# Delta rule: inverses and output weights pass through DRAM rings, decays are made by ScalarE

## The chip, the cores and the metric

The program runs on one core of one Trainium2 chip. The metric is device time in microseconds (us), from the first to the last instruction of the core and the little that lies around it. The engines are TensorE (PE in the profile; PEld are its weight loads), VectorE (DVE), ScalarE (ACT), GpSimd (POOL) and SyncE (SP). SP does no arithmetic: it issues transfers (DMAs), in order, and waits before one whose data or place is not ready. ACT issues some DMAs too.

## The reference, cut to what matters

One layer of a hybrid backbone: 1024 latent tokens and 256 context tokens, width 1024. One projection feeds two branches. Branch B is a differential softmax attention of 8 heads; branch A, where the change lies, is a gated delta rule of 8 heads with keys and values of 128, run over the tokens in both directions. For each head and direction it goes chunk by chunk:

```python
gc = jnp.cumsum(chunks(g), axis=-1)
decay = jnp.where(incl, jnp.exp(jnp.where(incl, gc[..., :, None] - gc[..., None, :], 0.0)), 0.0)
a_mat = jnp.where(strict, jnp.einsum('nbhid,nbhjd->nbhij', kc * bc[..., None], kc) * decay, 0.0)
t_mat = lax.linalg.triangular_solve(eye + a_mat, jnp.broadcast_to(eye, a_mat.shape), left_side=True, lower=True)
...
qk = jnp.where(incl, jnp.einsum('nbhid,nbhjd->nbhij', qc, kc) * decay, 0.0)
...
def step(s, xs_i):
    v_new = u_i - jnp.einsum('bhck,bhkv->bhcv', w_i, s)
    s_next = s * jnp.exp(gl_i)[..., None, None] + jnp.einsum('bhck,bhcv->bhkv', kd_i, v_new)
    o = jnp.einsum('bhck,bhkv->bhcv', qd_i, s) + jnp.einsum('bhij,bhjv->bhiv', qk_i, v_new)
```

The inverse of each chunk (`t_mat`) and the output weights (`qk`) don't depend on the state and can be made ahead of the scan over the chunks. Afterwards both branches are normed, gated, projected, merged and projected again.

## The kernel before

The kernel takes chunks of 128 tokens: 10 of them (`NT`), of which 8 are latent (`NL`). It runs in this order: norm and modulation, the projections of attention, of keys and of values (to about 660 us), then the delta rule together with the rest of the projections, then attention, and at the end the output projections.

In the delta-rule part (`run`, lines 721 to 741) several streams (Python generators) each yield one instruction at a time with its engine, an assumed duration and what it depends on. `flow` (line 86) takes the stream whose next instruction could start first, by assumed clocks of the engines, and so writes out a fixed order for PE, DVE, ACT, POOL and SP. On the chip each engine then works through its list in order and waits where a value is late. A DMA is assumed to take its own duration after the one before it and 2.0 us more. The streams:

- `scan(0)` and `scan(1)` (line 1180): the two directions, one head after the other, ten chunks each. A chunk is a chain of PE (`kT`, state S), DVE (`r`), PE (the inverse, `X[:, d, c]`), ACT (`vd`), PE (`kk`), DVE (new S). `out_chunk` (line 1227) makes the chunk's output from `qT`, `qk` and S in a queue of its own.
- `preps(0)` and `preps(1)` (line 1006): preparation of the even and of the odd heads, `gdn_prep` (line 1011). Steps: loads of a row of `gc`, spread over the partitions, into X (L1022), of kT and qT (L1024, L1025); decays in X: direction 0 by ten DVE steps (L1033), direction 1 by two POOL operations (L1028, L1030), then Exp of each; Gram products on PE, and their products with the decays on DVE, into `qk` and X (L1052, L1056); the diagonal blocks of 32 x 32 through DRAM (`da`, L1066 to L1079) to a layout with one block per partition, 31 steps of substitution on DVE (L1084, L1086), and back through DRAM (`db`, L1088, L1094); the merge of the block inverses to 64 and 128 by small matmuls (`pz`, `p2`, `p3`, `pz6`, `pu6`) with copies and memsets into X (L1104 to L1164); the scaling by beta (L1167); loads of kk and vv (L1174, L1175).
- `tails` (line 1248): norm and gate of a head's output; it ends with two stores.
- The filler: the projections of 6 query columns and of 32 gate columns, 48 matmuls each (`fill_flow`, tile `mm`), whose weights ACT loads and ACT and POOL split into two parts (`wh`, `wl`, L827 to L833). The filler has the lowest priority, and what is left of it when the last tail is done runs while attention begins (`rest`, line 155).

Each of the two pools `gh[0]` and `gh[1]` holds X, qk, kT and qT of one head, from the loads to the end of its scan. So `preps` waits for `min(self.scanned) > h - 2`: both directions of head h - 2 must be scanned. Two flags (`busy`, `merging`) let only one head at a time be in the substitution and one in the merge.

```python
yield lambda: self.gh[s] and C_Q + h * P in self.filled and min(self.scanned) > h - 2
```

Of the kernel before, what the change touches and what calls it, by code (L numbers as in the profile page):

```python
# [8 lines left out]
F32 = mybir.dt.float32  # L9
# [16 lines left out]
H = 8  # L26
# [33 lines left out]
class Block:  # L60
# [136 lines left out]
    def setup(self):  # L197
# [31 lines left out]
        self.ma = self.dp.tile([KT, P, L], F32, name="ma")  # L229
        self.gcd = self.dp.tile([2 * H, LT], F32, name="gcd")  # L230
# [437 lines left out]
    def run(self):  # L668
# [4 lines left out]
        with ExitStack() as left:  # L673
            self.hp, self.hs = self.spool(left, "hp"), {}
            self.hgroup(0)
            with ExitStack() as lw, ExitStack() as cx:
# [13 lines left out]
                with ExitStack() as sv:  # L690
# [30 lines left out]
                    with tc.manual_schedule(engines={E.PE, E.DVE, E.Activation, E.Pool, E.SP}):  # L721
# [243 lines left out]
    def gdn_first(self, st, keep):  # L965
# [3 lines left out]
        self.banks, self.busy, self.merging = [], False, False  # L969
        self.gs = None  # L970
        self.over, self.kvover, self.zring = {}, [[], []], [[], []]
        self.aT, self.ready, self.scanned, self.read, self.tailed = {}, {}, [0, 0], [0, 0], 0
        self.outq = [[], []]
# [32 lines left out]
    def preps(self, s):  # L1006
        for h in range(s, H, 2):
            yield lambda: self.gh[s] and C_Q + h * P in self.filled and min(self.scanned) > h - 2
            yield from self.gdn_prep(h)

    def gdn_prep(self, h):
# [3 lines left out]
        kT, qT = G("kT", [P, LT]), G("qT", [P, L])  # L1015
        X = G("X", [P, 2, NT, P])
        qk = G("qk", [P, 2, NL, P])
        ld = [None] * 2
        old = self.over.get(h - 2, [])
        for d in range(2):  # L1020
# [3 lines left out]
        tk = yield DMA, 1.82, old, lambda: nc.sync.dma_start(kT, self.gk[h])  # L1024
        tq = yield DMA, 1.46, old, lambda: nc.sync.dma_start(qT, self.gq[h])  # L1025
        te = [None] * 2
        g = H + h
        t = yield POOL, 2.28, [ld[1]], lambda: nc.gpsimd.tensor_tensor(  # L1028
            X[:, 1], self.gcc[:, :, g].unsqueeze(2).to_broadcast([P, NT, P]), X[:, 1], ALU.subtract)
        t = yield POOL, 2.84, [t], lambda: nc.gpsimd.tensor_tensor(X[:, 1], X[:, 1], self.sg.unsqueeze(1).to_broadcast(  # L1030
            [P, NT, P]), ALU.mult)
        for c in range(NT):
            t0 = yield DVE, 0.33, [ld[0]], lambda: V.scalar_tensor_tensor(X[:, 0, c], X[:, 0, c], self.gcc[:, c, h:h + 1],  # L1033
                                                                         self.sg, ALU.subtract, ALU.mult)
        te[0] = yield ACT, 1.16, [t0], lambda: nc.scalar.activation(X[:, 0], X[:, 0], AF.Exp), AF.Exp
        te[1] = yield ACT, 1.16, [t], lambda: nc.scalar.activation(X[:, 1], X[:, 1], AF.Exp), AF.Exp

        tX, tQ = [[], []], [[], []]
        for c0 in range(0, NT, 2):
# [10 lines left out]
            for d in range(2):  # L1050
                if c0 < NL:
                    t1 = yield DVE, 0.42, [t, te[d]], lambda: V.tensor_tensor(qk[:, d, c0:c0 + 2], pv[:, :, 1],  # L1052
# [17 lines left out]
        for d in range(2):  # L1070
            t = yield POOL, 2.303, tQ[d], lambda: nc.gpsimd.tensor_tensor(
                qk[:, d], qk[:, d], (self.up, self.lo)[d].unsqueeze(1).to_broadcast([P, NL, P]), ALU.mult)
            tQ[d] = t
        yield lambda: not self.busy
        self.busy = True
# [13 lines left out]
        self.busy = False  # L1089
        yield lambda: not self.merging  # L1090
        self.merging = True
# [4 lines left out]
        t64 = self.t64  # L1096
# [11 lines left out]
        self.banks.append(tz)  # L1108
        yield self.psum(2)
# [8 lines left out]
        tx = []  # L1118
        for m in range(4):
            tx += [(yield DVE, 0.48, [tt], lambda: V.tensor_copy(X[B(m), 0, :, B(m)], Rt[B(m), 0:NT]))]  # L1120
            tx += [(yield ACT, 0.46, [tt], lambda: nc.scalar.copy(X[B(m), 1, :, B(m)], R[B(m), NT:]))]
        for (b1, b2) in ((0, 1), (2, 3)):
            tx += [(yield POOL, 0.41, [tz], lambda: nc.gpsimd.memset(X[B(b2), 0, :, B(b1)], 0.0))]
            tx += [(yield POOL, 0.41, [tz], lambda: nc.gpsimd.memset(X[B(b1), 1, :, B(b2)], 0.0))]
# [6 lines left out]
        tx.append(t)  # L1131
        self.banks.append(t)
# [3 lines left out]
        for (m, q, f) in ((0, slice(0, 32), R[B(0), 0:NT]), (1, slice(32, 64), R[B(1), 0:NT]), (2, slice(0, 32), Rt[B(2), NT:]),  # L1136
                          (3, slice(32, 64), Rt[B(3), NT:])):
            t6 += [(yield DVE, 0.36, [tt], lambda: V.tensor_copy(t64[B(m), :, q], f))]
# [31 lines left out]
        self.merging = False  # L1170
        yield lambda: self.gs and (h == 0 or min(self.read) >= h - 1)
        kk, vv = (self.gs.tile([P, NT, P], F32, tag=n, name=n) for n in ("kk", "vv"))
        yield lambda: h == 0 or min(self.read) >= h
# [692 lines left out]
```

## Time and profile before

| | us |
|---|---|
| three runs | 2163.01, 2168.39, 2171.24; median 2168.39 |
| the profiled execution, its own time | 2171.22 |
| its span, first to last instruction | 2169.4 |
| PE busy | 2031.0 (94%) |
| DVE, ACT, POOL busy | 1494.5 (69%), 965.1 (44%), 988.0 (46%) |
| moved by DMA | 300.77 MB, mean 139 GB/s |

The profile times every instruction of one execution. "Busy" is time in which an engine executes; waiting, branching and issuing a DMA do not count. PEclk is the share of full clock that TensorE was granted. In a row of the time line stand start, duration, engine, line, operation, what it writes `<-` what it reads, and in brackets how long the engine was idle before and what released it. A row of the waits gives the waiting and the releasing instruction, total us, times, and the longest. Most matmuls are issued by one helper, so their line is L71, and the name of the tile tells them apart. Matmuls overlap each other: their rate is read from their starts.

### The profile page before, as it was taken

Reading aid. Unit: us, or ns where it says so; the run is one execution under the profiler, and the core shown is the slowest. Engines: PE = TensorE matmul, PEld = TensorE weight load, DVE = VectorE, ACT = ScalarE, POOL = GpSimd, SP = SyncE. Lnnn points to the kernel's source line nnn. Section 1 sums busy time; section 2 is a strip of 40 time slices with the busy share of each in tenths; the row PEclk is TensorE's granted clock in tenths of the full one; section 3 lists DMA queues with packets and bytes.
Section 4 is the critical chain, followed back from the end, with each engine's and each line's share of the span. In section 5 each row is a group of like instructions: output and inputs, shape, how many; then the busy total and the mean of one; then the engine's idle time right before and its main releaser. Section 6 shows DMA issues by size and latency. Waiting matters only on the chain. (4 is left out here: it accounts for less than half of the span.)

```text
span 2169.4 us, 37611 instructions
## 1 busy us (share of the span) xinstructions
PE 2031.0 (94%) x14207; PEld 1704.1 (79%) x14207; DVE 1494.5 (69%) x3492; ACT 965.1 (44%) x1979; POOL 988.0 (46%) x685
## 2 busy tenths in 40 slices
PE   8999999998899688888999899899999999999999
PEld 4999998887798577767787678686777777777899
DVE  4867776876777787885868767335788888873532
ACT  4322222434432344544355345246777777773210
POOL 2265663132335425443453433434776676775122
PEclk9999999999999799989999999999999999999999
DMA  9323335666665324334344432627455466217443
GB/s 318 97 80 127 108 107 176 169 167 173 189 173 156 98 79 124 109 113 126 98 144 128 131 118 86 189 88 226 105 143 139 129 165 176 93 55 255 145 143 97
DMA packets 351304, 300.77 MB, mean 139 GB/s; under 512 B 140063, under 2 KB 299393, under 8 KB 351123
## 3 DMA queue, kind: packets, MB, share of 16 engines
q1 hardware_dynamic: 304867, 254.85, 40.1%
q10 hardware_dynamic: 46256, 43.52, 6.4%
q8 instruction: 112, 1.84, 0.4%
q14 instruction: 69, 0.57, 0.1%
HBM read 200.64 MB, written 97.68 MB: 138 GB/s over the span
## 5 line engine op out<-in xcount | busy, mean ns | idle before, releaser
L71 PE MATMUL mm<-hs,wh 128*128 128x512 f32 x1216 | 435.9, 423 | 0.8 <-ACT zo L907 0.8
L454 PE MATMUL mm<-wh,hs 128*128 128x256 f32 (+1 forms) x1632 | 305.5, 287 | 0.4 <-DVE abt L656 0.3
L1384 DVE TENSOR_SCALAR_CACHE_REDUCE S<-s 128x512 f32<-128x512 f32 (+1 forms) x384 | 223.2, 597 | 108.7 <-PE s L71 107.9
L71 PEld LDWEIGHTS mm<-hs,wh 128*128 128x128 f32 x1216 | 235.7, 198 | 43.3 <-issue 1.4
L71 PE MATMUL mm<-hs,wl 128*128 128x512 f32 x608 | 256.6, 422 | 8.8 <-POOL wl L833 8.8
L454 PEld LDWEIGHTS mm<-wh,hs 128*128 128x128 f32 x1632 | 258.3, 193 | 1.1 <-DVE abt L656 0.6
L431 PE MATMUL mm<-hs,wh 128*128 128x512 f32 (+1 forms) x832 | 227.8, 361 | 14.2 <-ACT xc L471 14.2
L1414 POOL TENSOR_TENSOR S<-S 128x1280 f32<-128x1280 f32 x64 | 188.6, 2947 | 111.6 <-ACT S L1409 109.1
L454 PE MATMUL mm<-wl,hs 128*128 128x256 f32 (+1 forms) x816 | 232.9, 286 | 0.0
L833 POOL TENSOR_TENSOR wl<-wr,wh 128x512 fp32r<-128x512 f32 x74 | 107.7, 1476 | 175.4 <-ACT wh L832 147.6
L431 PEld LDWEIGHTS mm<-hs,wh 128*128 128x128 f32 x832 | 149.4, 192 | 40.2 <-ACT xc L471 17.0
L1395 ACT ACTIVATE S<-S,mn 128x1280 f32<-128x1280 f32 x128 | 175.0, 1367 | 12.4 <-DVE mn L1388 11.6
L454 PEld LDWEIGHTS mm<-wl,hs 128*128 128x128 f32 x816 | 157.3, 193 | 0.0
L431 PE MATMUL mm<-hs,wl 128*128 128x512 f32 (+1 forms) x416 | 149.7, 360 | 0.0
L71 PEld LDWEIGHTS mm<-hs,wl 128*128 128x128 f32 x608 | 119.9, 197 | 29.5 <-POOL wl L833 9.3
L1430 ACT CAST ah<-t 128x512 fp32r<-128x512 f32 (+1 forms) x192 | 98.3, 513 | 98.8 <-PE t L74 96.2
L71 PE MATMUL s<-kh,qs 128*128 128x512 f32 (+1 forms) x384 | 133.2, 386 | 1.0 <-DVE S L1384 0.8
L476 DVE SCALAR_TENSOR_TENSOR ac<-xc,smallT,ac 128x1284 f32<-128x1284 f32 (+1 forms) x72 | 122.0, 1695 | 12.8 <-ACT ac L472 10.8
L1084 DVE TENSOR_TENSOR tmp<-ab,ts 80x31 f32<-80x31 f32 (+15 forms) x248 | 107.9, 435 | 16.6 <-DMA ab<-da 11.6
L1437 DVE TENSOR_TENSOR al<-t,ah 128x512 fp32r<-128x512 f32 (+1 forms) x192 | 113.6, 592 | 7.8 <-ACT ah L1430 7.3
L74 PE MATMUL t<-ct,S 128*128 128x128 f32 x640 | 101.9, 273 | 8.1 <-DVE al L1437 7.2
L1086 DVE TENSOR_TENSOR ts<-ts,tmp 80x31 f32<-80x31 f32 (+15 forms) x248 | 103.7, 418 | 4.8
(317 smaller groups left out, 5070.6 us busy)
## 6 DMA issues: line engine op xcount, KB each, us to landing
wr<-in_w_in_dram SPq DMA_DIRECT2D x21, 1024.0 KB
wr<-in_w_in_dram ACTq DMA_DIRECT2D x37, 512.0 KB
X<-gcd SPq DMA_DIRECT2D x16, 640.0 KB
kh<-kd SPq DMA_DIRECT2D x32, 320.0 KB
wa<-in_w_ada_dram SPq DMA_DIRECT2D x8, 1024.0 KB
qd<-col SPq DMA_DIRECT2D x16, 512.0 KB
kd<-col SPq DMA_DIRECT2D x16, 512.0 KB
gt<-zo ACTq DMA_DIRECT2D x16, 512.0 KB
```

The source lines that it names most:

```text
L71: self.nc.tensor.matmul(out, lhsT, rhs, start=start, stop=stop)
L74: self.nc.tensor.transpose(out, src, self.ident[:src.shape[0], :src.shape[0]])
L431: nc.tensor.matmul(pt[:, :n], wt[:, k, cs], ht[:, k, o:o + n], start=i == 0, stop=i == 3 * KT - 1)
L454: nc.tensor.matmul(pt[:, j * W:j * W + n], ht[:, k, ts], wt[:, k, :n], start=i == 0, stop=i == 3 * KT - 1)
L476: nc.vector.scalar_tensor_tensor(ac[:, w], xc[:, o + j:o + j + wd // parts], self.convw(j, ct), ac[:, w], ALU.mult, ALU.add)
L833: t2 = yield POOL, 1.36, [t1], lambda: nc.gpsimd.tensor_tensor(lo[:, k], raw[:, k], hi[:, k].bitcast(F32), ALU.subtract)
L1084: t = yield DVE, n * w / 960.0 + 0.11, [t, t1], lambda: V.tensor_tensor(tv, ab[:, j + 1:, j:j + 1].to_broadcast([80, n, w]), ts[:, j, :w]. ...
L1086: t = yield DVE, n * w / 960.0 + 0.11, [t, t1], lambda: V.tensor_tensor(ts[:, j + 1:, :w], ts[:, j + 1:, :w], tv, ALU.subtract)
L1384: self.nc.vector.tensor_scalar(x[c][:, o:o + m], x["s", j, c][:, :m], 1.0, None, ALU.mult, ALU.min, accum_out=x["m3"][:, c, j:j + 1])
L1395: self.nc.scalar.activation(S, S, AF.Exp, bias=x["mn"][:, c:c + 1], scale=-1.0, accum_out=w["l0"][:, c, t:t + 1])
L1414: self.nc.gpsimd.tensor_tensor(x[0], x[0], x[1], ALU.add)
L1437: self.nc.vector.tensor_tensor(y["al", k][:, :, q], x["t", k][:, :nb * P].rearrange("p (j f) -> p j f", f=P), y["ah", k][:, :, q].bitcast( ...
```

## The change

- The decays: for each head and direction ten ScalarE `Abs` (of the loaded row less `gc` of the partition) and one `Exp` with scale -1, in place of the subtraction and the sign on DVE and POOL.
- After the merge each half of X (five chunks, both directions) is stored to `xd` in DRAM, and `qk`, once masked, to `qkd`. The new streams `loads(0)` and `loads(1)` bring them back for the scans in units of two chunks, in rings of two units for each direction; `used_` tells when a unit has been read.
- The new stream `sets` loads the scan's own keys and queries (`sk`, `sq`) with kk and vv, once the head before has been scanned. The kT, qT and qk of preparation lie in `gh[0]` only, one head at a time (`gram`, `kT_t`, `qk_t`); `gh[1]` holds X and the output.
- Preparation of head h waits for `stored > h - 2`. Counters (`subst`, `merge`, `gram`) replace the flags and put the heads in order.
- The masking of qk on POOL (`masked`) and the copies of block inverses into X and t64 (`placed`) run as streams of their own (`asides`), and the four copies out of `p2` depend on its matmuls only.

```diff
@@ run
-    (self.preps(1), 3), (self.tails(), 3), (self.forever(self.convs), 4)):
+    (self.preps(1), 3), (self.tails(), 3), (self.sets(), 3), (self.loads(0), 3), (self.loads(1), 3), (self.forever(self.convs), 4), (self.forever(self.asides[0]), 3),
+    (self.forever(self.asides[1]), 3)):
@@ preps
-            yield lambda: self.gh[s] and C_Q + h * P in self.filled and min(self.scanned) > h - 2
+            yield lambda: self.gh[s] and C_Q + h * P in self.filled and self.stored > h - 2
@@ gdn_prep
-        t = yield POOL, 2.28, [ld[1]], lambda: nc.gpsimd.tensor_tensor(
-            X[:, 1], self.gcc[:, :, g].unsqueeze(2).to_broadcast([P, NT, P]), X[:, 1], ALU.subtract)
-        t = yield POOL, 2.84, [t], lambda: nc.gpsimd.tensor_tensor(X[:, 1], X[:, 1], self.sg.unsqueeze(1).to_broadcast(
-            [P, NT, P]), ALU.mult)
-        for c in range(NT):
-            t0 = yield DVE, 0.33, [ld[0]], lambda: V.scalar_tensor_tensor(X[:, 0, c], X[:, 0, c], self.gcc[:, c, h:h + 1],
-                                                                         self.sg, ALU.subtract, ALU.mult)
-        te[0] = yield ACT, 1.16, [t0], lambda: nc.scalar.activation(X[:, 0], X[:, 0], AF.Exp), AF.Exp
-        te[1] = yield ACT, 1.16, [t], lambda: nc.scalar.activation(X[:, 1], X[:, 1], AF.Exp), AF.Exp
+        for d in range(2):
+            for c in range(NT):
+                t = yield ACT, 0.265, [ld[d]], lambda: nc.scalar.activation(
+                    X[:, d, c], X[:, d, c], AF.Abs, bias=self.gcc[:, c, d * H + h:d * H + h + 1], scale=-1.0)
+            te[d] = yield ACT, 1.18, [t], lambda: nc.scalar.activation(X[:, d], X[:, d], AF.Exp, scale=-1.0), AF.Exp
+        yield lambda: self.gram == h
...
-        yield lambda: not self.busy
-        self.busy = True
+        self.kT_t = [tX[1][-1], list(tQ)]
+        self.asides[0].append(self.masked(h, qk, tQ))
+        yield lambda: self.subst == h
...
-                    t = yield DVE, 0.5, [t], lambda: V.tensor_copy(X[B(r), d, :, B(q)], p2[B(r)])
+                    tx += [(yield DVE, 0.5, [e], lambda: V.tensor_copy(X[B(r), d, :, B(q)], p2[B(r)]))]
                 else:
-                    t = yield ACT, 0.43, [t], lambda: nc.scalar.copy(X[B(r), d, :, B(q)], p2[B(r)])
+                    tx += [(yield ACT, 0.43, [e], lambda: nc.scalar.copy(X[B(r), d, :, B(q)], p2[B(r)]))]
...
+            self.store_t.setdefault(h, []).append((yield DMA, 2.2, ends, lambda: nc.sync.dma_start(
+                self.xd[h][:, :, cs], X[:, :, cs])))
+        self.merge = self.stored = h + 1
+
+    def masked(self, h, qk, tQ):
+        nc, t = self.nc, [None] * 2
+        for d in range(2):
+            t[d] = yield POOL, 2.303, tQ[d], lambda: nc.gpsimd.tensor_tensor(
+                qk[:, d], qk[:, d], (self.up, self.lo)[d].unsqueeze(1).to_broadcast([P, NL, P]), ALU.mult)
+        t = yield DMA, 3.1, t, lambda: nc.sync.dma_start(self.qkd[h].rearrange("p d c f -> p (d c f)"),
+                                                       qk.rearrange("p d c f -> p (d c f)"))
+        self.store_t.setdefault(h, []).append(t)
+        self.qk_t, self.gram = [t], h + 1
...
+    def sets(self):
+        for h in range(H):
+            yield lambda: self.gs and min(self.scanned) >= h and self.tailed >= h - 1 and C_Q + h * P in self.filled
...
+            for n, src in (("sk", self.gk[h]), ("kk", self.gkk[h]), ("vv", self.gv[h]), ("sq", self.gq[h])):
...
+                w["t" + n] = yield DMA, 1.82, free, lambda: nc.sync.dma_start(
+                    o, src.rearrange("(c p) f -> p c f", p=P) if n == "vv" else src)
+
+    def loads(self, d):
+        nc, i = self.nc, 0
+        order = ((8, 0, 2, 4, 6), (8, 6, 4, 2, 0))[d]
+        for h in range(H):
+            for c in order:
+                yield lambda: self.gs and self.stored > h and len(self.used_[d]) > i - 2
+                u = {}
+                for n, src in (("x", self.xd), ("qk", self.qkd))[:2 if c < NL else 1]:
+                    u[n] = x = self.gs.tile([P, 2, P], F32, tag=f"{n}{d}", name=n, bufs=2)
+                    u["t" + n] = yield DMA, 0.45, [self.store_t[h], self.used_[d][i - 2] if i > 1 else None], \
+                        lambda: nc.sync.dma_start(x, src[h][:, d, c:c + 2])
+                self.units_[d, h, c] = u
+                i += 1
@@ scan
-                t = yield PE, 0.2235, [tr, w["tX"]], lambda: self.mm(pc[:, 1], X[:, d, c], r)
+                t = yield PE, 0.2235, [tr, u["tx"]], lambda: self.mm(pc[:, 1], u["x"][:, c % 2], r)
@@ out_chunk
-        t2 = yield PE, 0.2235, [tn, w["tqk"], b], lambda: self.mm(po[:, 1], w["qk"][:, d, c], vn)
+        t2 = yield PE, 0.2235, [tn, u["tqk"], b], lambda: self.mm(po[:, 1], u["qk"][:, c % 2], vn)
@@ tails
             if end:
+                yield lambda: self.stored == H
                 yield from self.att_load_ops(0)
```

More of the change, by code (lines that the diff above doesn't have):

```diff
@@ L1108, in gdn_prep @@
         self.banks.append(tz)
+        tZ.append(tz)
         yield self.psum(2)
@@ L1117, in gdn_prep @@
             t3 = yield PE, 0.02, [tz, b], lambda: self.mm(p3[B(2), c], Z[B(3), c], Rt[B(3), NT + c]), 0.25
[L1118 to L1124, printed above, removed]
+        tx, e = [], t
         for i, (b1, b2) in enumerate(((2, 3), (0, 1))):
@@ L1169, in gdn_prep @@
                 ends.append(t)
[L1170 to L1173, printed above, removed]
-        tkk = yield DMA, 1.82, self.kvover, lambda: nc.sync.dma_start(kk.rearrange("p c f -> p (c f)"), self.gkk[h])
-        tvv = yield DMA, 1.82, self.kvover, lambda: nc.sync.dma_start(vv, self.gv[h].rearrange("(c p) f -> p c f", p=P))
@@ new lines, in placed @@
+    def placed(self, X, R, Rt, tt, tz, out):
+        nc, V, t64 = self.nc, self.nc.vector, self.t64
+        B = lambda b: slice(32 * b, 32 * b + 32)
+        tx, t6 = [], []
+        for m in range(4):
+            tx += [(yield DVE, 0.48, [tt], lambda: V.tensor_copy(X[B(m), 0, :, B(m)], Rt[B(m), 0:NT]))]
+            tx += [(yield ACT, 0.46, [tt], lambda: nc.scalar.copy(X[B(m), 1, :, B(m)], R[B(m), NT:]))]
+        for (m, q, f) in ((0, slice(0, 32), R[B(0), 0:NT]), (1, slice(32, 64), R[B(1), 0:NT]), (2, slice(0, 32), Rt[B(2), NT:]),
+                          (3, slice(32, 64), Rt[B(3), NT:])):
+            t6 += [(yield DVE, 0.36, [tt], lambda: V.tensor_copy(t64[B(m), :, q], f))]
+        yield lambda: tz
+        for (b1, b2) in ((0, 1), (2, 3)):
+            tx += [(yield POOL, 0.41, tz, lambda: nc.gpsimd.memset(X[B(b2), 0, :, B(b1)], 0.0))]
+            tx += [(yield POOL, 0.41, tz, lambda: nc.gpsimd.memset(X[B(b1), 1, :, B(b2)], 0.0))]
+        out += [tx, t6]
```

84 lines of the change are left out of this document (48 added, 36 removed).

## The prediction

> **What bounds the kernel now.** I read four views: the stages, the reasons for which TensorE (PE) sat idle, the waits of SP's queue, and the time line around the largest stall. First the stages: the delta rule with its filler, its last part, and the attention.
>
> ```profile
> span 2169.4 us, 37611 instructions
> PEclk9999999999999799989999999999999999999999
> ...
> core 0: us, PE busy (x) PEld busy (x) DVE busy (x) ACT busy (x) POOL busy (x), PEclk, DMA share, GB/s
> 680.00:760.00 80.00, 59.11 (x499) 47.91 (x498) 65.66 (x151) 29.43 (x43) 39.60 (x29) 0.81 0.40 117
> 760.00:1440.00 680.00, 617.56 (x5087) 513.47 (x5085) 482.58 (x1279) 299.59 (x777) 286.14 (x280) 0.95 0.39 117
> 1440.00:1500.00 60.00, 59.22 (x266) 45.13 (x265) 14.78 (x52) 26.93 (x50) 22.80 (x15) 1.00 0.60 169
> 1500.00:1952.00 452.00, 441.12 (x2683) 329.07 (x2682) 365.44 (x1187) 331.87 (x549) 315.48 (x153) 1.00 0.47 133
> ...
> 1440.00:1500.00 60.00, 51.39 (x208) 1.00 0.60 169
> ```
>
> The last row is the third stretch for the filler's matmuls (`mm`) alone. The scans end near 1440 us, and the filler still has 51.39 us of PE work left; it then runs with PE full (59.22 of 60) at clock 1.00. So the delta-rule part does not end when its scans end: it ends when PE has done its work. The change adds and removes no matmul, so only PE's losses can move: idle time, 80 - 59.11 = 20.9 us and 680 - 617.56 = 62.4 us, and slow clock, 0.19 x 80 = 15 us and 0.05 x 680 = 34 us. Together 132 us at most (the two overlap a little). That is the ceiling of any gain here.
>
> Where does PE sit idle, and what holds preparation?
>
> ```profile
> PE pu L71 <- DVE Z L1152: 13.6, 6, 5.3
> PE oT L74 <- POOL oa L1273: 10.6, 2, 5.9
> PE p L71 <- issue: 9.0, 3, 4.2
> PE mm L71 <- POOL wl L833: 8.8, 1, 8.8
> PE pz L71 <- DVE RR L1095: 7.4, 2, 5.2
> PE chain L71 <- DVE S L1221: 6.5, 7, 2.6
> PE pz L71 <- issue: 5.5, 1, 5.5
> ...
> SPq L1088 <- DVE ts L1086: 190.7, 8, 51.4
> ...
> SPq L1022 <- PE chain L71: 78.9, 4, 39.9
> ...
> SPq L1022 <- PE out L71: 51.1, 2, 27.7
> ...
> L1219 DVE COPY S<-chain x16: 279/282/293, 768.2 to 1410.9; 128x128 f32<-128x128 f32 x16
> ```
>
> Columns of a wait: total us, times, longest. The long idle times belong to the merges (pz, p, pu: 13.6 + 9.0 + 7.4 + 5.5 = 35.5 us), one tail (oT) and one weight split (wl); the scans' own waits are short. SP waits 78.9 + 51.1 = 130 us for scans before it may issue the load of a decay buffer (L1022): preparation of head h+2 starts only after the scan of head h. The first state copies of the heads (L1219) run from 768.2 to 1410.9 us: 642.7 / 7 = 92 us a head. The last head shows the loop:
>
> ```profile
> 1277.18 0.81 SPq L1022 DMA_DIRECT2D X<-gcd  x2
> ...
> 1328.06 4.65 DMA da<-cb
> 1332.78 3.16 DMA ab<-da
> ...
> 1399.20 10.20 PE mm L71 x44
> 1409.40 0.45 PE chain L71 x4
> ...
> 1441.14 13.40 PE mm L71 x59
> ```
>
> Its preparation takes 1409.4 - 1277.2 = 132 us and its scan 32 us. Two buffers take turns, so a mean cycle of 92 us means 184 us for preparation and scan of one buffer.
>
> **The change part by part.** (a) *Decays.* Per head it removes ten DVE steps (L1033) and two POOL operations (L1028, L1030) and adds twenty ScalarE Abs of 128x128; the two Exp stay.
>
> ```profile
> 692.42 2.49 POOL L1028 TENSOR_TENSOR X<-gcc,X 128x1280 f32<-128x1280 f32 x1 [2.71 <-DVE ts L1086]
> 694.99 3.01 POOL L1030 TENSOR_TENSOR X<-X,sg 128x1280 f32<-128x1280 f32 x1
> 698.85 13.59 POOL L833 TENSOR_TENSOR wl<-wr,wh 128x512 fp32r<-128x512 f32 x2 [0.86 <-ACT wh L832]
> ...
> 692.28 0.42 DVE L1084 TENSOR_TENSOR tmp<-ab,ts 80x256 f32<-80x256 f32 x1
> 692.73 2.46 DVE L1086 TENSOR_TENSOR ts<-ts,tmp 80x256 f32<-80x256 f32 x1
> 695.22 3.05 DVE L1084 TENSOR_TENSOR tmp<-ab,ts 80x255 f32<-80x255 f32 x1
> ...
> 711.27 0.80 PE L71 MATMUL mm<-hs,wl 128*128 128x512 f32 x1 [8.83 <-POOL wl L833]
> 711.86 1.05 PE L71 MATMUL mm<-hs,wh 128*128 128x512 f32 x2
> ...
> 714.42 1.05 PE L71 MATMUL mm<-hs,wh 128*128 128x512 f32 x2
> ...
> 1292.22 2.47 POOL L833 TENSOR_TENSOR wl<-wr,wh 128x512 fp32r<-128x512 f32 x2
> ...
> 1009.64 2.71 DVE L1033 SCALAR_TENSOR_TENSOR X<-X,gcc,sg 128x128 f32<-128x128 f32 x10
> ...
> L1208 ACT ACTIVATE vd<-chain,edk 128x128 f32<-128x128 f32 x144 | 51.7, 368 | 78.8 <-PE chain L71 78.2 <-ACT vn L1212 0.2 <-ACT oa L1238 0.2
> ```
>
> Two substitution steps of DVE that take 0.42 us apart took 2.46 and 3.05 us beside these two POOL operations: 4.7 us lost a head, and 2.7 us for L1033 itself (ten in 2.71). The other way round, while L1033 and the query convolution kept DVE full, two weight splits on POOL took 13.59 us, where a pair takes 2.47 at another place; PE waited 8.83 us, and its next matmuls came 0.43 us apart (six from 711.86 to 714.42) instead of 0.23 (59 in 13.40 us, above). The slow stretch adds an estimated 2 us: ten to twelve matmuls at 0.2 us more. ScalarE pays at most 20 x 0.368 = 7.4 us a head (from L1208, the same shape with an operand per partition), 59 us for eight: hidden, since ScalarE is busy 299.6 of 680 us. Uncovered, it would lengthen a preparation by that less the 5.5 us that the two POOL operations took.
>
> The Trainium skill, SBUF — State Buffer (Who interferes with whom), says that DVE and GpSimd share one pair of ports as an exclusive lock, and that a DVE instruction with two SBUF inputs is shut out by a GpSimd instruction that reads SBUF, but not one with a single SBUF input. The 2.46 us above agrees; by the rule nothing of the scans' DVE steps, which read PSUM and one SBUF tile, is relieved, and the term (a2) below would be nearer its small end, at -8, for a sum of 2151 us instead of 2143.
>
> The start (a1), 680 to 760 us: with two POOL operations fewer before the split, I take 8 of the 11 us (8.8 + 2) back; bounds 0 and -11. The heads (a2): 7.4 us less DVE for each of seven heads is 52 us; DVE is the longest of the side engines there (482.6 of 680), yet PE is kept going by filler, so I take less than a third, -16; bounds 0 and -52.
>
> (b) *Buffers.* X goes to DRAM after the merge and comes back in rings of two chunks; so preparation h+2 waits for the store of X by h, no longer for the scan of h. The loop of one buffer loses a scan of 32 us and gains a store, taken as the 4.65 us of `da<-cb`: (184 - 32 + 5) / 2 = 78.5 us a head. DVE needs 482.6 / 680 x 92 = 65 us a head, 7.4 less after (a), 58: under 78, but near enough that I take 80. The scan stage becomes 7 x 12 = 84 us shorter, and the filler that it no longer covers runs after it with PE full, as 1440:1500 shows. The loss rate was (62.4 + 34) / 680 = 14%, so 84 us fewer of such a stage save 12 us; bounds -40 (the loss halves, as merges find scan work beside them) and +30 (the same stalls packed closer, and 5% more).
>
> (c) *Traffic.* Per head X (1.31 MB) and qk (1.05 MB) are written and read back, and kT and qT are loaded twice: 5.9 MB, 47 MB in all, with 18 loads, 3 stores and 2 reloads: 23 issues on SP, 184 in all. SP's issues take 0.3 to 0.45 us, so 55 to 83 us of a queue that waits most of the time. The engines moved 362 GB/s where they were full:
>
> ```profile
> 1284.00:1288.00 4.00, 4.00 (x35) 3.11 (x34) 0.91 (x2) 2.23 (x10) 3.95 (x4) 1.00 1.05 362
> ...
> DMA packets 111185, 96.74 MB, mean 121 GB/s; under 512 B 42339, under 2 KB 93539, under 8 KB 111113
> ```
>
> so 47 MB cost 130 us of transfer beside the 0.39 share now: room enough. A ring load has the time of one unit, 6.4 us (two of ten chunks in 32 us), and lands like `ab<-da` in 3.2 us. It is on the path only at a head's first unit or where SP holds it. I take 1 us of PE a head, +8; bounds 0 and +88 (below).
>
> (d) *Merge order.* The copies into X and t64 move to a stream of their own and the four copies out of p2 no longer wait for each other: no instruction more. Part of (b)'s low bound; 0.
>
> Sum against the profiled execution (2171.2 us for a span of 2169.4; the runs' median is 2168.4, 3 lower): -8 - 16 - 12 + 8 = -28, that is 2143, and 2140 beside the median. I say 2142.
>
> **The rivals.** *Long stalls go (2107).* The merges now have another head's scan beside them, so that PE's long waits become short. The five long kinds above (pu, oT, p, wl, pz twice) are 54.9 us and the slow clock 49; half of both is 52, with 12 of (b): 2171 - 64 = 2107. For it: the scans' own waits are at most 2.6 us each. Against it: a merge's chain from DVE to PE and back is as long as before.
> The Trainium skill, TensorE: Matmul & The Clock Gate (Part 1), puts the slow clock down to idle windows of about 3.4 us; by that rule stalls of 2 us cost their own time only, and all 49 us of clock could go, for about 2110 us. The trace fits it at 711 us, after the 8.83 us stall.
>
> *Nothing is gained (2165).* The order of PE is written out beforehand and its losses come from steps that run later than ordered; with scan, two preparations and merge closer together, DVE (58 of 80 us) is as late as before and the 132 us only move. Only (a1) stays: 2171 - 8 + 2. The same comes out if the new counters (one Gram part, one substitution, one merge at a time) hold preparation where the scan held it.
>
> *Ring loads behind SP (slower, 2209).* SP issues in order. Its store after the substitution (L1088) holds it 190.7 us in 8 waits, up to 51.4 us. Today nothing inside a scan hangs on SP; afterwards nine loads of each direction and head do, and one ordered behind a late L1088 stops the scan's matmul on PE and the filler behind it. Such a stop costs what the 8.83 us one did, 11 us with its clock. In six of eight heads: 66 - 28 = +38, 2209; in all eight 88 - 28 = +60, 2231. It decides from the third stop on (28 / 11).
> The Trainium skill, DMA: Bandwidth & Descriptors (Anatomy of one DMA), gives a DMA about 2 us of fixed cost, most of it the receipt of the write, longest towards HBM; a way through DRAM pays it twice, an estimate of 4 us a head by the page. The rows have 4.65 + 3.16 us for such a pair.
>
> **How the numbers follow.** Chances: forecast 0.40, long stalls go 0.15, nothing gained 0.15, SP 0.30. A measurement here tells 0.5% (11 us) from no change. Faster: 0.37 of the forecast's 0.40, the 0.15, and 0.01: 0.53. Same: 0.03 + 0.13 = 0.16. Slower: 0.30 + 0.01 = 0.31. The forecast's own range is 2120 to 2163. For 8 in 10 I reach down to 2095 (most of the 2107 case) and up to 2200 (half of the slower case).
>
> **What would show it.** Right: no L1028, L1030, L1033; substitution steps near 0.42 us; the first state copies under 85 us apart; SP no longer waiting for the chain at the decay load; after the last scan more than 51 us of filler with PE full; PE's idle time in the stage under 83 us. Wrong: new rows of PE waiting for x or qk from DRAM with several us each (SP), a clock under 0.9 over the stage, or heads 90 us apart (counters). If DVE is over 85% busy and PE waits for it, (b) was too hopeful; if the long merge waits are gone, (b) was too careful.

## The result, and the profile after

The changed kernel takes 2167.3 us (median of 20 runs, 2156.7 to 2174.7) against 2166.6 us before (20 runs): ratio 1.0001, 95% interval 0.9988 to 1.0014. The forecast was 2142; its rival "nothing is gained" had 2165. The profiled execution is the slowest of the 20 (2174.7 us). One execution of a kernel further down (keys buffered once) took 3173 us at a granted clock of 0.556; the medians are without it.

The windows of the changed kernel, columns as before (stretch; busy us of PE, its weight loads, DVE, ACT, POOL; granted clock; DMA share; GB/s):

```profile
680.00:760.00 80.00, 72.78 (x551) 58.16 (x549) 69.17 (x167) 33.46 (x61) 22.19 (x26) 0.91 0.58 179
760.00:1440.00 680.00, 624.23 (x5111) 521.28 (x5107) 459.57 (x1181) 333.06 (x888) 260.62 (x266) 0.95 0.58 183
1440.00:1500.00 60.00, 58.15 (x253) 41.38 (x251) 23.58 (x83) 27.20 (x62) 21.84 (x18) 0.84 0.63 187
1480.00:1500.00 20.00, 19.09 (x50) 9.63 (x49) 12.69 (x50) 12.21 (x17) 9.58 (x4) 0.52 1.07 321
```

PE's idle time in the stage fell from 83.3 to 7.2 + 55.8 = 63.0 us, and DVE has 23 us less. But 1480 to 1500 is new: PE counts as busy, at clock 0.52. The time line of PE shows why:

```profile
1474.74 0.39 PE L71 MATMUL mm<-hs,wl 128*128 128x512 f32 x1
1474.97 0.62 PE L71 MATMUL s<-kh,qs 128*128 128x512 f32 x2
...
1493.69 1.06 PE L74 MATMUL t<-ct,S 128*128 128x128 f32 x4
```

The last filler matmul (`mm`) starts at 1474.7, 24 us earlier than before (1498.5). Attention's first scores (`s`) then run alone for 18.7 us, until the first transposes (`t`) follow; before, filler covered this. So of 24 us only 6 arrive at the first `t` (1499.7 before). No long stall precedes the slow clock: the longest idle gap of PE between 1474.7 and 1493.7 us is 0.48 us.

The rest of the difference lies at the end. Most of the lead is kept until the last scores of attention (4.7 us earlier than before), and the rest, mostly the output projections, which the change does not touch, takes 234.6 us instead of 226.5. Over all profiled executions of this document it takes 225.5 to 234.6 us, so these 8 us are not read as an effect of the change.

The waits of the changed kernel, 680 to 1500 us (total, times, longest), PE's and then SP's:

```profile
PE pu L71 <- DVE Z L1151: 12.2, 5, 4.4
PE pq L71 <- DVE qss L954: 10.2, 3, 4.3
PE chain L71 <- DMA x<-xd: 9.2, 4, 4.2
PE chain L71 <- ACT vd L1262: 6.2, 4, 4.5
...
SPq L1227 <- PE chain L71: 112.2, 41, 10.6
SPq L1348 <- POOL oa L1346: 100.8, 12, 27.8
SPq L1169 <- POOL X L1166: 81.8, 11, 16.6
SPq L1093 <- DVE ts L1091: 29.0, 5, 18.9
```

The stall at the weight split is gone, the merge waits (`pu`) are not. Scans now wait for X from DRAM. SP no longer sits before the store of the substitution (29.0 instead of 190.7 us) but before ring loads whose place is not free (L1227) and stores of X (L1169); it waits for the tails' stores (L1348) as it did before (173.3 us at L1291).

From the same traces, head by head: the preparation (first load of X to last beta; mean of heads 2 to 7), the gap from the last beta to the scan's first matmul (all heads), the gap from the last beta to the next load of X into that buffer, the scan's length, the distance of the scans' starts, and the end of the last scan:

```
                    prep   beta>scan  beta>next X  scan   apart  last scan ends
before             145.1      2.1        39.2      36.3    91.8      1440
after              167.4     19.9         6.8      42.4    88.9      1449
```

### The profile page after: what moved, and what is told of

It reads as the page before. It is cut to its first block, busy times and chain, and to the rows that moved or that the text cites. A ratio compares the mean times of both kernels' runs of the same rounds, so it can differ in the third digit from the quotient of the medians.

```text
span 2172.9 us, 37989 instructions
## 1 busy us (share of the span) xinstructions
PE 2051.0 (94%) x14207; PEld 1719.1 (79%) x14207; DVE 1480.2 (68%) x3412; ACT 1003.2 (46%) x2133; POOL 938.1 (43%) x669
## 5 line engine op out<-in xcount | busy, mean ns | idle before, releaser
L71 PE MATMUL mm<-hs,wh 128*128 128x512 f32 x1216 | 421.5, 418 | 2.0 <-ACT zo L910 1.8
L71 PEld LDWEIGHTS mm<-hs,wh 128*128 128x128 f32 x1216 | 234.6, 196 | 44.7 <-ACT zo L910 2.4
L433 PE MATMUL mm<-hs,wh 128*128 128x512 f32 (+1 forms) x832 | 230.9, 365 | 13.9 <-ACT xc L473 13.9
L433 PEld LDWEIGHTS mm<-hs,wh 128*128 128x128 f32 x832 | 151.8, 195 | 39.9 <-ACT xc L473 16.5
L71 PE MATMUL s<-kh,qs 128*128 128x512 f32 (+1 forms) x384 | 139.5, 403 | 2.6 <-DVE S L1441 2.4
L1089 DVE TENSOR_TENSOR tmp<-ab,ts 80x31 f32<-80x31 f32 (+15 forms) x248 | 116.6, 470 | 16.3 <-DMA ab<-da 10.4
L1091 DVE TENSOR_TENSOR ts<-ts,tmp 80x31 f32<-80x31 f32 (+15 forms) x248 | 121.7, 491 | 6.1
```

Of the source, the lines that this page charges most:

```text
L71: self.nc.tensor.matmul(out, lhsT, rhs, start=start, stop=stop)
L433: nc.tensor.matmul(pt[:, :n], wt[:, k, cs], ht[:, k, o:o + n], start=i == 0, stop=i == 3 * KT - 1)
L1089: t = yield DVE, n * w / 960.0 + 0.11, [t, t1], lambda: V.tensor_tensor(tv, ab[:, j + 1:, j:j + 1].to_broadcast([80, n, w]), ts[:, j, :w]. ...
L1091: t = yield DVE, n * w / 960.0 + 0.11, [t, t1], lambda: V.tensor_tensor(ts[:, j + 1:, :w], ts[:, j + 1:, :w], tv, ALU.subtract)
```

## The experiments

All times below are set beside the kernel before in the same series of runs (its medians were 2167.2, 2165.1, 2167.6 and 2168.5), so that a difference is one of medians.

### The two halves: decays alone, rings alone

The kernel before with the new decays and nothing else; and, the other way round, the changed kernel with the old decays (the same diff, reversed).

```diff
-        t = yield POOL, 2.28, [ld[1]], lambda: nc.gpsimd.tensor_tensor(
...
-        te[1] = yield ACT, 1.16, [t], lambda: nc.scalar.activation(X[:, 1], X[:, 1], AF.Exp), AF.Exp
+        for d in range(2):
+            for c in range(NT):
+                t = yield ACT, 0.265, [ld[d]], lambda: nc.scalar.activation(
+                    X[:, d, c], X[:, d, c], AF.Abs, bias=self.gcc[:, c, d * H + h:d * H + h + 1], scale=-1.0)
+            te[d] = yield ACT, 1.18, [t], lambda: nc.scalar.activation(X[:, d], X[:, d], AF.Exp, scale=-1.0), AF.Exp
```

> The kernel before with the decays alone moved to ScalarE (Abs, then Exp); buffers, waits and merges as before. Forecast's step (a): the weight split at 702 to 711 us no longer stalls PE and DVE has 7.4 us less a head, so -8 - 16 = -24 us: 2143. Theory A (PE's losses follow from the written order; what one engine is relieved of moves to the next wait): the stall at 711 us goes, but the heads stay 90 to 93 us apart and the time is 2155 to 2168. Theory B (the relief is real and the ring loads ate it in the full change): 2140 to 2150 here.

> The changed kernel with the decays as before on DVE and POOL (L1028, L1030, L1033 of before); rings, buffers, waits and merges as changed. Forecast's steps (b) and (c): -12 + 8, that is 2163, with heads 80 us apart. Theory A (the preparation takes longer beside a scan and a second preparation, so heads stay near 90 us apart, and the losses only move): 2160 to 2175, first scan some 25 us later than before. Theory B (ring loads cost the scans time): over 2175, with PE waiting 10 us or more for x or qk from DRAM.

Decays alone: 2145.8, **-21.4** (ratio 0.9896, 0.9877 to 0.9915). Rings alone: 2192.6, **+25.4** (1.0114, 1.0093 to 1.0135). So the change is a gain and a loss of about the same size. With the rings alone heads are 89.4 us apart, not the 80 of the forecast. The windows of the kernel with the decays alone:

```profile
680.00:760.00 80.00, 72.99 (x584) 58.47 (x583) 73.18 (x171) 34.81 (x65) 30.12 (x31) 0.95 0.48 140
760.00:1440.00 680.00, 629.49 (x5195) 524.81 (x5194) 419.54 (x1196) 343.25 (x918) 262.13 (x272) 0.97 0.41 120
```

DVE has 63 us less in the long stretch than before (482.6), PE is idle for 50.5 instead of 62.4 us and its clock is 0.97 instead of 0.95; in the first stretch 7.0 instead of 20.9 us, clock 0.95 instead of 0.81. Heads stay 90.7 us apart: what shrinks is PE's loss, not the cycle. The last filler matmul starts at 1449.7 us, 49 us earlier than before, but attention's first `t` only 33 us earlier (1466.9): as in the change, nothing covers attention's start.

```profile
1460.00:1480.00 20.00, 19.55 (x64) 10.78 (x64) 13.81 (x52) 12.79 (x19) 13.26 (x6) 0.60 1.09 307
```

### The wait put back

```diff
-  yield lambda: self.gh[s] and C_Q + h * P in self.filled and self.stored > h - 2
+  yield lambda: self.gh[s] and C_Q + h * P in self.filled and self.stored > h - 2 and min(self.scanned) > h - 2
```

> The changed kernel with one wait put back: the preparation of head h+2 starts only after both scans of head h, as before the change. Forecast's step (b), that this wait set the 92 us a head: heads go back to 92 us, +12 us, 2179. Theory A (the wait was only one bound; without it the preparation takes as much longer as it starts earlier): 2160 to 2174, preparations of 140 to 150 us instead of 167, heads 88 to 94 us apart.

2179.4, +12.2 (1.0058, 1.0042 to 1.0075). Removing the wait is worth about 12 us, as the forecast's (b) had it; a later section shows that a change of the order alone can move a kernel by nearly as much. The signs were those of theory A: preparation takes 140.7 us with the wait and 167.4 without, and heads are 90.6 and 88.9 us apart. With the wait, the rings and the merge order cost 12.2 + 21.4 = **34 us** beside the decays alone, where the forecast had 8.

### Filler held back for attention's start

```diff
-  yield lambda: i in self.split_
+  yield lambda: i in self.split_ and (i < 35 or self.tailed == H)
```

> The changed kernel with the last three units of the filler held back until the last tail is done; nothing else. Theory A, second half (the filler ends 24 us earlier than before, but scans and tails end 8 us later, so the first 19 us of attention run with PE half idle and at clock 0.52): these units cover the attention's start, 10 to 19 us less: 2148 to 2157, and the clock of 1480 to 1500 us back near 1.00. Rival (the time is PE's work plus losses that lie elsewhere, so moving filler moves nothing): 2163 to 2170.

2176.7, +9.4 (1.0033, 1.0016 to 1.005): outside both ranges. Attention's start is covered, but the filler is now missing where the last tail is late, and PE stands for 8.9 us there:

```profile
PE oT L74 <- POOL oa L1330: 14.1, 3, 8.9
```

### What in the rings costs

Four kernels between "decays alone" and "rings with the wait". X kept in its buffer, as a diff against the change with the wait:

```diff
-            self.store_t.setdefault(h, []).append((yield DMA, 2.2, ends, lambda: nc.sync.dma_start(
-                self.xd[h][:, :, cs], X[:, :, cs])))
...
-                t = yield PE, 0.2235, [tr, u["tx"]], lambda: self.mm(pc[:, 1], u["x"][:, c % 2], r)
+                t = yield PE, 0.2235, [tr, tX], lambda: self.mm(pc[:, 1], X[:, d, c], r)
```

X and qk both kept, against that one (left of the rings are the single key buffer of the Gram part, the second load of keys and queries, and the merge order):

```diff
-        t = yield DMA, 3.1, t, lambda: nc.sync.dma_start(self.qkd[h].rearrange("p d c f -> p (d c f)"),
...
-        t2 = yield PE, 0.2235, [tn, u["tqk"], b], lambda: self.mm(po[:, 1], u["qk"][:, c % 2], vn)
+        t2 = yield PE, 0.2235, [tn, self.qks[h][1], b], lambda: self.mm(po[:, 1], self.qks[h][0][:, d, c], vn)
```

The merge order alone, on top of the decays, is the change's `placed` stream and its `tx += [...]` lines. The stores that nobody reads, on top of the decays:

```diff
+        yield DMA, 3.1, tQ, lambda: nc.sync.dma_start(self.qkd[h].rearrange("p d c f -> p (d c f)"),
...
+            yield DMA, 2.2, ends[:], lambda: nc.sync.dma_start(self.xd[h][:, :, cs], X[:, :, cs])
```

> The changed kernel in which X stays in its buffer: no store of X and no ring loads of X, the scans read X where the merge wrote it, and preparation waits for the scan again; qk still goes through DRAM in its ring, the keys are loaded twice, the merge has its new order. Beside the same kernel with X in DRAM (2179 with this wait) it tells what the way of X through DRAM costs. Theory C (the 33 us that the rings cost beside the kernel with the new decays alone lie in X's way: a first unit stored and loaded before each scan, and loads behind SP's waits): 2145 to 2158, first scan near 770 us, scans 36 us long. Theory D (they lie in the rest: SP's queue and PE's order with qk, the keys and the merge): 2168 to 2180.

> The kernel before with the new decays and with the new merge order (the copies into X and t64 as a stream of their own, the four copies out of p2 no longer one after the other); buffers as before, no rings. Forecast's step (d): 0 beside the new decays alone (2146). Theory C: 2140 to 2150. Theory D: 2155 or more, with merge waits (pu, p) back over 8 us in all.

> The kernel before with the new decays, which also writes X and qk of each head to DRAM after the merge and the mask, where nothing reads them: 19 MB and three issues a head on SP, each waiting for POOL. It tells what stores and SP's added waits cost without any load of a ring. Forecast's step (c) has 8 us for all traffic and issues, so 2146 to 2152. Theory D (SP held by stores delays the loads of the next preparation): 2155 to 2170.

> The changed kernel with X and qk both kept in their buffers (no way through DRAM, no ring) and the scan's wait back; left of the rings are the single key and query buffer of the Gram part, the second load of keys and queries for the scans, and the new merge order. Beside X kept alone (2167) it tells what qk's way through DRAM costs, beside the new decays with the new merge (2149) what the keys' second load costs. Theory F (qk's ring loads hold SP up to 47 us and everything behind them): 2146 to 2155. Rival G (the single key buffer and the second loads): 2160 to 2170.

Differences to the kernel before, with the 95% interval of the ratio:

```
decays alone                          2145.8   -21.4   0.9877-0.9915
 + merge order                        2149.5   -15.6   0.9916-0.9945
 + keys buffered once, loaded twice   2160.0    -8.5   0.9936-0.9971
 + qk through DRAM                    2167.5    +2.4   0.9989-1.0028
 + X through DRAM                     2179.4   +12.2   1.0042-1.0075
 - wait for the scan (the change)     2167.3    +0.8   0.9988-1.0014
decays + stores nobody reads          2179.4   +14.3   1.0044-1.0084
```

No single part carries the 34 us: the steps are 6, 7, 11 and 10. Neither theory C (X's way, 33) nor F (qk's ring, most of it) holds as stated. The stores that nobody reads cost 36 us beside the decays alone, more than either expectation for them. Here is one head of that kernel, SP's queue and then the scan's first matmul:

```profile
1058.49 10.66 SPq L1169 DMA_DIRECT2D xd<-X  x2
1069.19 0.61 SPq L1174 DMA_DIRECT2D kk<-gkk  x1
1069.84 0.95 SPq L1175 DMA_DIRECT2D vv<-gv  x1
...
1078.71 0.68 PE L71 MATMUL chain<-vv,X 128*128 128x128 f32 x4 [0.23 <-DMA vv<-gv]
```

SP waits for POOL's beta to issue X's second store, and the loads of kk and vv, which need neither, are issued behind it; the scan waits for vv. On average the scan starts 10.6 us after the last beta instead of 4.3, and heads are 96.2 instead of 90.7 us apart. The loads go out late because of their place in a queue. From the issue of vv to the matmul another 8.9 us pass, with the store of X and the load of kk ahead of it; how much of this is their bytes was not separated, nor what the store of qk holds up.

### The loads' order

In the changed kernel, head 3 (timeline of POOL, SP and PE):

```profile
1041.96 2.87 POOL L1166 TENSOR_TENSOR X<-X,beta 128x640 f32<-128x640 f32 x2
...
1044.86 0.52 SPq L1169 DMA_DIRECT2D xd<-X  x1
1048.34 0.80 SPq L1024 DMA_DIRECT2D X<-gcd  x2
1049.18 0.43 SPq L1030 DMA_DIRECT2D kT<-gk  x1
1049.65 0.69 SPq L1031 DMA_DIRECT2D qT<-gq  x1
1050.38 1.32 SPq L1227 DMA_DIRECT2D x<-xd  x2
...
1062.42 0.38 PE L71 MATMUL chain<-vv,x 128*128 128x128 f32 x2
```

The store at 1044.86 frees X's buffer, and so releases preparation h+2. Its four loads (2.5 MB) are issued ahead of the two of 128 KB on which the scan waits. From 1050 to 1062 us the DMA engines are full (share 1.00, the last column but one):

```profile
1050.00:1062.00 12.00, 12.00 (x57) 9.94 (x56) 10.36 (x29) 1.51 (x3) 1.48 (x1) 1.00 1.00 344
```

So the scan starts 17.6 us after the last beta (1044.8). Two edits, each a kernel of its own, tell the collision from the way itself: preparation h+2 also waits until the first ring loads of head h are placed; or the first ring load waits for the store of its half of X alone.

```diff
-  yield lambda: ... and self.stored > h - 2
+  yield lambda: ... and self.stored > h - 2 and all((d, h - 2, 8) in self.units_ for d in range(2) if h > 1)
...
-  yield lambda: self.gs and self.stored > h and len(self.used_[d]) > i - 2
+  yield lambda: self.gs and (self.half if c == 8 else self.stored) > h and len(self.used_[d]) > i - 2
...
-  u["t" + n] = yield DMA, 0.45, [self.store_t[h], ...
+  u["t" + n] = yield DMA, 0.45, [self.store_t[h][:2] if c == 8 else self.store_t[h], ...
```

> The changed kernel in which the loads for the preparation of head h+2 (two decay halves, keys, queries: 2.4 MB) are put on SP behind the first ring loads of head h instead of ahead of them. In the changed kernel's trace the last beta of a head and the first matmul of its scan lie 14.5 to 20 us apart (36 once), before the change 0 to 5; SP issues the four big loads first, and the DMA engines are full when the ring loads follow. Theory E (this collision, not the stores' and loads' own latency, makes the scans late): the distance falls to 7 to 12 us, and the time by 5 to 10, to 2157 to 2162. Rival (PE's losses lie elsewhere, a later scan only moves filler): 2164 to 2172 with the distance as short.

> The changed kernel in which the first ring load of each direction (chunks 8 and 9) waits only for the first half of X to be stored, not for both; the halves are stored 7 to 21 us apart, and the first unit lies in the half that comes first. Theory E: the scans' first matmuls come 8 to 15 us earlier against the last beta, and the time falls by 8 to 15 us, to 2152 to 2160. Rival (as above): 2164 to 2172.

Ring loads first: 2151.9, -15.7 (0.9928, 0.9906 to 0.995), 16.5 better than the change and more than the 5 to 10 expected. Head 3 there:

```profile
1037.04 0.53 SPq L1169 DMA_DIRECT2D xd<-X  x1
1037.60 6.65 SPq L1227 DMA_DIRECT2D x<-xd  x2
...
1045.98 0.92 SPq L1024 DMA_DIRECT2D X<-gcd  x2
...
1047.37 0.39 PE L71 MATMUL chain<-vv,x 128*128 128x128 f32 x2
```

The scan starts 10.4 us after the last beta; over all heads it is 10.6 instead of 19.9, and the last scan ends at 1432 instead of 1449. Most of what is left here is the second ring load, which SP holds for 5.7 us until the store has landed. Half first: 2161.6, -6.0 (0.9952 to 0.9985). Its scans start 3.5 us after the last beta, yet take 46.9 us instead of 42.4: they start early and then take longer. Heads are as far apart as with the ring loads first (87.8 and 87.9 us), so the 10 us between the two kernels are not explained by the scans; they are within the scatter of the order, below.

### Ring loads on ScalarE's queue

```diff
-                    u["t" + n] = yield DMA, 0.45, [...], lambda: nc.sync.dma_start(x, src[h][:, d, c:c + 2])
+                    u["t" + n] = yield ADMA, 0.45, [...], lambda: nc.scalar.dma_start(x, src[h][:, d, c:c + 2])
```

> The changed kernel with the ring loads issued by ScalarE's queue instead of SP's; all else as changed. Theory F (SP, held 140 us by ring loads that wait for a free place, delays the loads of the preparations and the tails): 2145 to 2158, SP's waits for the chain gone. Rival (the loads' place and the bandwidth count, not the queue; or ScalarE is now held instead): 2162 to 2185.

2191.6, +23.1 (1.0116, 1.0094 to 1.0139). PE now waits for ScalarE's step of the scan (6.2 us in the change). First PE's waits, then ScalarE's time line at the longest of them:

```profile
PE chain L71 <- ACT vd L1262: 33.4, 9, 12.1
```

```profile
784.11 0.33 ACTq L1227 DMA_DIRECT2D x<-xd  x1
784.47 1.14 ACT L835 CAST wh<-wr 128x512 fp32r<-128x512 f32 x2 [11.65 <-DMA qk<-qkd]
786.71 0.33 ACTq L1227 DMA_DIRECT2D x<-xd  x1
788.61 0.33 ACTq L1227 DMA_DIRECT2D qk<-qkd  x1
788.98 1.57 ACT L1040 ACTIVATE X<-X,gcc 128x128 f32<-128x128 f32 x5 [3.37 <-DMA kT<-gk]
...
794.49 0.35 ACT L1262 ACTIVATE vd<-chain,edk 128x128 f32<-128x128 f32 x1
```

ScalarE stands for 11.65 us until a ring load can go (to 784.47), and later for 3.37 us; what is ordered behind, a cast, the next head's decays and `vd` at the end, comes late, and the scan waits for `vd`. The ring loads' waits for the chain on SP (112.2 us) are gone, as theory F expected; the time that it expected did not come, and the loss is larger than the rival's, too. The run does not show what a queue without other duties would give.

### How much is the order alone

One assumed duration of the written order, that of the scan's second matmul, is changed; the instructions stay the same.

```diff
-  t = yield PE, 0.2235, [tr, ...
+  t = yield PE, 0.225, [tr, ...
```

> The kernel with the new decays alone, and one assumed duration of the order written beforehand (the scan's second matmul) 0.225 instead of 0.2235 us: the same instructions, in a slightly different order on each engine. It tells how much of any difference here is the order alone. If the -21 us of the new decays are their work: within 6 us of 2146. If they are luck of the order: 2152 to 2170.

> The changed kernel with the assumed duration of the scan's second matmul 0.225 instead of 0.2235 us in the order written beforehand, as in the run with the new decays alone, where this moved the time by -8 us. How much of +0 us is the order: if the effects found so far (-21 to -27 for the decays, +34 for the rings, -12 for the wait) are larger than the order's own scatter, this comes within 8 us of 2167.

> The kernel before with the same 0.225. The order written beforehand hardly changes here, so 2163 to 2170; beyond 8 us from 2166 the scatter of the order is as large as the effects.

> The changed kernel with the ring loads of head h ahead of the preparation's loads of head h+2, as in the run that came to 2152, with 0.225 instead of 0.2235 us assumed for the scan's second matmul in the order written beforehand. If the 15 us are the loads' order: 2146 to 2158, beside 2162 for the changed kernel with the same 0.225. If they are scatter: 2158 to 2168.

```
                 0.2235    0.225
before              0      -0.9
decays alone     -21.4    -27.4
the change        +0.8     -5.9
ring first       -15.7    -26.9
```

Two of the four expectations held; the decays alone and the ring loads first came out faster than expected (2137.6 and 2141.6). The order alone moves a kernel by up to 11 us. The decays (-21, -27), the rings with the wait (+34, one order only) and the loads' order (-17, -21) stand above it; the steps of 6 to 11 in the ladder and the 12 us of the wait do not stand alone. Beside the decays alone the change loses 22.2 us under one order and 21.5 under the other; with the ring loads first it loses 5.7 and 0.5. The fastest kernel of all, at 2137.6 (0.9873, 0.9854 to 0.9892), is the one with the decays alone and 0.225; it has no rings. With the loads in the right order the rings come up to the decays alone (-15.7 and -26.9 beside -21.4 and -27.4), and not past them.

## Why the prediction was wrong

**What bounds the kernel** was right: the stage ends with PE's work plus its losses. One item was overlooked: the filler also covers attention's start. Where no filler is left when attention's scores begin, 17 to 19 us of scores alone follow (1474.7 to 1493.7 in the change, 1449.7 to 1466.9 with the decays alone), at a clock of 0.52 and 0.60 in the rows above. In the kernel with the decays and 0.225, filler lasts to 1453.1 and `t` starts at 1454.3: filler 3 us later than with 0.2235, `t` 13 us earlier. The one run that tried to use this, with filler held back, lost more elsewhere, so its worth is read from these times alone.

**(a) Decays, -24: the sum was right**, -21.4 alone and -27.4 under the other order, **its parts were too small, and luck made up for it.** PE's idle time in 680 to 760 us fell by 13.9 us, more than the 11 allowed as the start's bound, and the clock there rose from 0.81 to 0.95. Filler ended 49 us earlier in all, and 16 of these were lost again where nothing covers attention's start, a cost that the prediction did not have.

**(b) Buffers, -12: the size came out, the mechanism half, so the agreement is partly luck; it is also hardly larger than the scatter of the order.** The scan did leave the loop: from beta to the next load 39.2 became 6.8 us (forecast: 32 less, 5 more). But the step held the preparation constant at 152 us, and it grew from 145 to 167. Heads are 88.9 us apart, not 80. Against the kernel with the wait put back (140.7) preparation is 26.7 us longer, spread over its parts: the Gram products take 26.2 us instead of 16.8, the substitution 44.3 instead of 33.9, the merge 35.4 instead of 30.5; the pauses before substitution and merge are 4 and 3 us longer, the start 6 us shorter (means of heads 2 to 7). The substitution shows a cause (lines view, 760 to 1440 us; busy us and mean ns of a step): with the wait put back,

```profile
L1089 DVE TENSOR_TENSOR tmp<-ab,ts 80x112 f32<-80x112 f32 (+15 forms) x200 | 84.4, 422 | 14.5 <-DMA ab<-da 6.1 <-POOL X L1160 3.7
L1091 DVE TENSOR_TENSOR ts<-ts,tmp 80x112 f32<-80x112 f32 (+15 forms) x200 | 81.7, 408 | 4.7
```

and in the change,

```profile
L1091 DVE TENSOR_TENSOR ts<-ts,tmp 80x247 f32<-80x247 f32 (+15 forms) x205 | 103.9, 507 | 5.3
L1089 DVE TENSOR_TENSOR tmp<-ab,ts 80x252 f32<-80x252 f32 (+15 forms) x204 | 99.3, 487 | 11.6 <-DMA ab<-da 6.6
```

A step takes 80 ns longer. An estimate of the loss takes for each of the 62 steps of a head a low duration over all kernels as its own: of 496 steps in the change, the 330 that run beside no POOL operation lose 2.7 us in all, the 166 others 73 us; with the wait put back the sum is 44 instead of 76 us. By the operation that lies longest beside a step, two operations of the tails stand for 16.5 us instead of 1.0, betas for 19.0 instead of 11.8, weight splits for 31.5 instead of 25.4, masks for 3.7 instead of 1.2: without the wait more of the other heads' work on POOL falls into the substitution. Thirty steps beside memsets lost 0.2 us together. That is 32 us, 4 a head; why the Gram products and the merge take longer is not settled. The Trainium skill, SBUF — State Buffer (Who interferes with whom), states that a DVE instruction with two SBUF inputs contends with a GpSimd instruction that reads SBUF; the split of 2.7 and 73 us agrees with it. The prediction's smaller end for (a2) by that rule, -8 and so -16 for (a), lies below both measurements.

**(c) Traffic and ring loads, +8: this is the step that failed.** With (d) it is 34. Volume was right (143.6 MB instead of 96.7 from 680 to 1480 us, 47 more), and the engines had room on average. What failed is the price: a load "is on the path only at a head's first unit", at 1 us a head. The first unit alone delays each scan by 18 us (2.1 to 19.9). Of these, 9.3 are its place behind the loads that the same store releases, and 8.5 remain with the ring loads first, for the store, its landing and the load, where the step counted the 3.2 us of a load in a free queue. Putting the ring loads first takes back 17 us of time (21 under the other order), most of what the change loses beside the decays alone (22.2 and 21.5). The rest of the 34 was narrowed, not settled: steps of 6 to 11 us for merge order, keys and qk, each within the order's scatter.

**(d) Merge order, 0**: +5.8, within the scatter; nothing shown against it.

**The rivals.** "Nothing is gained" has the number and not the reason: the relief of DVE did not move elsewhere, it was paid back by the rings. Its second reason, that the new counters hold preparation, is not borne out: in the change each head's substitution starts 8 to 75 us after the end of the one before, each Gram part 33 us or more, each merge 31 or more. "Ring loads behind SP" saw the right kind of cost at a wrong place: SP's store of the substitution holds it for 29.0 us instead of 190.7, and the queue that counts is that of the next preparation's loads. "Long stalls go" came half true: the rows that it counted fell from 54.9 to 20.5 us (`pu` 12.2, oT and p 3.7 and 3.6, wl 0.8, pz 0.2), but waits for `pq` (10.2), for x from DRAM (9.2) and for `vd` (6.2) came in their place, and `pu` itself stayed.

**The signs.** Right: no L1028, L1030, L1033; SP no longer waits for the chain at the decay load; idle under 83 us. Wrong: substitution steps longer, not near 0.42 us; heads not under 85 us apart; after the last scan (1449) 26 us of filler, not over 51. Two of the signs against came true: heads 89 us apart, though not by the counters, and a PE row waiting for x from DRAM.

## What to carry to other kernels

A transfer that frees a buffer also releases the next user's loads: on an in-order queue ask which of them the nearest consumer needs, and issue those first. A change with several parts that measures as nothing should be split before it is dropped, for here one half was worth 21 to 27 us. And where an order is written out from assumed durations, run a version that differs in nothing but one duration by under a per cent: it gives a size below which a difference explains nothing.

## What was not expected of the hardware

What the collision of DVE and POOL costs in a sequence of short steps: 166 substitution steps beside POOL operations lost 73 us, 0.44 us each, as long as a step itself, and 30 of them, beside memsets, lost 0.2 us together. And PE can count as busy for 95% of 20 us (19.09), with no idle gap above 0.48 us, at a granted clock of 0.52. Whether the POOL half or the DVE half of the old decays brought the gain was not tried.
